# Where the passes over the output weights, some sums and the last two rows stand in a hybrid attention and RG-LRU block

## The chip, the cores and the metric

The kernel runs on one NeuronCore of a Trainium2 chip. The metric is the device time of one execution in microseconds; the kernel before takes 917.62 us (median of three runs, 917.18 to 918.01). The engines are called by short names: PE is TensorE, DVE VectorE, ACT ScalarE, POOL GpSimd and SP SyncE. Each engine works through its own instructions strictly in the order in which the program lists them, because the kernel switches the automatic ordering off (`manual_schedule`) and writes the order out by hand. Transfers are issued on SP's queue or on POOL's, a few on ACT's.

## The reference

The reference computes one layer of a hybrid block over 1024 positions and 1024 channels, all in float32. Cut to what matters here:

```
h      = rmsnorm(x, norm_g) * (1 + scale) + shift          # scale, shift, gate from c @ w_ada + b_ada
q, k, v, g_attn, xr, g_rnn, m_attn, m_rnn = split(h @ w_in)
y_attn = sliding_window_attention_with_sinks(rope(q), rope(k), v) * silu(g_attn)
y_rnn  = rg_lru(causal_depthwise_conv(xr)) * silu(g_rnn)
merged = sigmoid(m_attn) * (y_attn @ w_attn_proj) + sigmoid(m_rnn) * (y_rnn @ w_rnn_proj)
x      = x + gate * (merged @ w_out)
out    = rmsnorm(x, final_g)
```

The change touches the preparation of `w_out`, the product `merged @ w_out`, and the last normalisation.

## The kernel before, in words

**Products.** A float32 operand is split into a high part (rounded by ACT, a "cast") and a low part (the remainder, a subtraction on DVE, a "rest"); a product is three matmuls: high by high, low by high, high by low. The large products `h @ w_in` and `merged @ w_out` are made by a Strassen-Winograd scheme, seven block products in the place of eight, on operands that are sums of blocks.

**Stages.** After a start-up the projection runs as 22 `Pair`s of 128 output columns each, seven slots per pair, twelve matmuls per slot (line 694). A planner (`run`, `background`, `put`) walks through the slots; besides the fixed steps of a pair it takes steps from three waiting lists and puts each one where its own estimate of ACT's and DVE's load (`Load`) leaves room. A callable entry in a list holds the list back until it returns true. The last pair and the product with `w_rnn_proj` are woven into attention (a loop over `u` from 0 to 34). Then comes the product with `w_attn_proj` in eight chunks `c` of 48 matmuls (`ap_k`), with the merging of each chunk behind it: `merge1` and `merge2` on DVE, `naturals` (high and low part of a merged chunk), `sums` (Strassen sums of merged chunks `kc` and `kc + 4`). Beside it `prep_r` makes the cast and the rest of the next chunk's weights, which PE needs before it can start that chunk. The product with `w_out` follows, 24 groups `n` of 12 matmuls and then a row-wise end (`products`, line 1864).

**The weight passes.** `out_weights` prepares `w_out` in eight passes, four values of `kc` by two column halves. A pass has four steps: `load` (two 256 KB transfers from `w_out` into tiles `t1`, `t2`, issued on POOL), `gated` (two multiplications by the gate on DVE, line 1179, and two stores on POOL), `one` (two subtractions, lines 1184 and 1185, and a store) and `two` (an addition and a subtraction, lines 1189 and 1190, and a store). There is one set of tiles, so a pass's `load` stands behind the pass before. The stores go to `wq_d` in memory, and the product with `w_out` reads them back (`load_b11`, `load_wr`). The passes stand at the end of the third waiting list. In front of `gated`, `one` and `two` stands the function `idle`; in front of `load` it does not stand, only a delay in slots. What is left of the list when the pairs end goes, without the callables, into `rest_out`, and `outs(n)` issues the next `n` steps from it, at once and in order. Before, it is called at three places: after attention (as many steps as leave a whole number of passes, then one more), after `naturals(0)`, and after `naturals` of the chunks `c` = 2, 3, 4.

**The end.** The first four row blocks `x1` and the last four `x2` take the banks `b1` and `b2` of `merged @ w_out` by additions on DVE (`add_x`, line 1869), are squared on ACT (line 1883) and scaled (`row1`, `scale2`). `prep_sum` makes high and low parts of a Strassen sum for later groups; `prep_right(n + 4)` does the same for the weights four groups ahead. `scale2` scales one row block: its second half on ACT (line 1911), its first half on DVE (line 1912), then two stores.

Of the kernel before, what the change touches and what calls it, by code (L numbers as in the profile page):

```python
# [52 lines left out]
def tile_hybrid_block(ctx, tc, x, x_t, pk, rows, posr, posi, c_row, w_ss, w_gate, w_main, w_v,  # L53
# [525 lines left out]
    W = {}  # L579
# [104 lines left out]


    SLOT, GATE = 2.75, 5.5
    ROOMY = (52, 56), (111, 117)

    def product(ps, w, b, first=True):
        h, l = w  # L690
# [95 lines left out]
    def flush():  # L786
        while behind:
            behind.pop(0)()
# [126 lines left out]
                "C22": (half(1), lambda s: []),  # L915
                "C21": lambda s: other(s) + [("N", 0, 0, lambda: conv(1)(s))]}

    gq, asks = [], []

    def gate_weights(hb, oc):  # L920

# [16 lines left out]
    def ask(hb, oc):  # L938

        if ("g", (hb, oc)) not in W and (hb, oc) not in gq:  # L940
            gq.append((hb, oc))
        return ("g", (hb, oc)) in W
# [7 lines left out]
    def start_gates(hb):  # L950

        load1, split1 = gate_weights(hb, 1)
        c0, c1 = after_gates(hb, 0), after_gates(hb, 1)
        asks.extend([lambda: ask(hb, 0), lambda: ask(hb, 1)])
        waiting[0].extend([lambda: "gate" in W, asks[-2]])
        if hb < 3:
            one, two = [], [asks[-1]]
            for todo, steps_ in ((one, c0), (two, c1)):
                for i, step in enumerate(steps_):
                    todo.extend(step + [slots(1)])  # L960
                    if todo is one and i == 1:
                        todo.append(lambda: second(hb))
            waiting[0].extend(one + two)
        else:
            gap = [None]
            for item in ([[lambda: W.setdefault("rush", True)], c0[0], gap, c0[1],
                          [lambda: second(hb)], c0[2], c0[3], gap, c0[4], c0[5], gap, c0[6],
                          [lambda: ask(hb, 1)], c1[0], c0[7], gap, c0[8], c1[1], c0[9], c1[2],
                          c1[3], gap, c1[4], c1[5], gap, c1[6], c1[7], gap, c1[8], c1[9]]):
                waiting[0].extend([slots(1)] if item is gap else item)  # L970
        waiting[1].extend([load1, slots(2)] + split1)
        return True
# [186 lines left out]


    def idle():
        t = W["slot"]
        return t < 130 and (not waiting[0] or waiting[0][0] in asks or (
            any(a <= t < b for a, b in ROOMY) and Load.dve <= Load.pe + 2.8))

    def out_weights(kc, cols):
        t1, t2, t3, t4 = wq
# [97 lines left out]
    def sink(u):  # L1265
        px = at.tile([P, 4, P + 1], F32, tag="p", name="p", bufs=3)
        U["p", u] = px, at.tile([P, 2, 4], F32, tag="small", name="small", bufs=4)
        gs = slice(u // 8 * 4, u // 8 * 4 + 4)
        return lambda: G.tensor_copy(px[:, :, P:P + 1], W["sink"][:, gs].unsqueeze(2))
# [336 lines left out]
    def outs(n):  # L1606
        for _ in range(min(n, len(rest_out))):
            put(rest_out.pop(0)[0])
# [27 lines left out]
    for u in range(32 + 3):  # L1636
        todo = (left - KEEP + (35 - u) // 2) // (35 - u)
        if u < 32:
            scores(u)
            maxima_a(u)  # L1640
            maxima_d(u)
        if 1 <= u < 33:
            weights_a(u - 1)
        low = [steps_[2] for steps_ in high]
        while high:
            high.pop(0)[1]()
        for _ in range(todo):
            piece()
        flush()
        if 1 <= u < 33:  # L1650
            weights_d(u - 1)
        if u >= 3:
            values(u - 3)
            join_a(u - 3)
            join_d(u - 3)
        if 2 <= u < 34:
            transposed(u - 2)
            split_a(u - 2)
            split_d(u - 2)
        if u + 1 < 32:  # L1660
            sink(u + 1)()
        if 2 <= u < 34:
            masks(u - 2)
        if "hpool" in W:
            for f in low:
                f()
            if late and ("gq", late[0]) in U and u >= loaded[late[0]] + 2:
                high.append(a_prep(late.pop(0)))
                high[0][0]()
        do_later()  # L1670
        if u >= 3 and u % 2 == 0:
            late.append((u - 3) // 2)
        if u >= 2 and len(loaded) < 16 and len(loaded) <= (u - 2) // 2 and (
                len(loaded) - (late[0] if late else (u - 2) // 2) < 2):
            m = len(loaded)
            load_gq(m)
            loaded[m] = u
# [4 lines left out]
    for m in late:  # L1682
        for f in a_prep(m):
            f()
    flush()
    at_ctx.close()
    psx_ctx.close()
    outs((len(rest_out) - 1) % 4 + 1)
    for _ in more:
        pass  # L1690
    outs(1)
    flush()
    load_r(10)
    prep_r(9, 0)
# [82 lines left out]

    first_w = []

    def load_b11():  # L1780
        for kc in range(4):
            first_w.append(load_half(wq_d[kc][:, 0, :]))

    def load_wr(n):
# [13 lines left out]
    load_r(KC + 3)  # L1798
    ap_k(0, range(6))
    prep_r(KC + 1, 1)  # L1800
    merge1(0)
    merge_loads(1)
    merge_load2(1)
# [11 lines left out]
    for c in range(2, KC):  # L1815
        ps[c] = new_ps()
        ap_k(c, range(KC))
        if c + 2 < KC:
            load_r(KC + c + 2)
        if c + 1 < KC:  # L1820
            for i in range(2):
                prep_r(KC + c + 1, i)
        merge1(c)
        if c + 1 < KC:
            merge_loads(c + 1)
        merge2(c - 1)
        if c + 1 < KC:
            merge_load2(c + 1)
        naturals(c - 1)
        if c < 5:  # L1830
            outs(4)
        if c > 5:
            for n in ((0,), (1, 2, 3))[c - 6]:
                prep_right(n, first_w[n])
        if c in (5, 6):
            sums(c - 5)
        if c == 5:
            load_b11()
    load_wr("B21")
    load_wr("NT1")  # L1840
    load_wr("B22")
# [67 lines left out]
    def scale2(i, f, eng=nc.sync):  # L1909
        a, b = x2[i]  # L1910
        A.activation(b, b, AF.Copy, scale=f[:, 3:4])
        V.scalar_tensor_tensor(out=a, in0=a, scalar=f[:, 3:4], in1=fg_bc[:, SL[0]], op0=MUL,
                               op1=MUL)
        t = (4 + i) * P
        dma(out[t:t + P, SL[1]], b, eng)
        dma(out[t:t + P, SL[0]], a)

    for n in range(24):
        p, kc = n // 4, n % 4
        for i in range(4):  # L1920
            products(p, kc, i)
        if n == 0:
            naturals(7)
            for i in range(4):
                load_x1(i, "ss" if i > 1 else "xo", 2)
            fg_bc = W["tout"].tile([P, S], F32, tag="rp", name="fg_bc")
            dma(fg_bc[:], rows[0:1, D:2 * D].to_broadcast([P, D]))
        if n == 3:
            for i in range(4):
                A.copy(b1[i], b2[i])  # L1930
        if n + 4 < 28:
            prep_right(n + 4)
        if n in (2, 4):
            sums(2 if n == 2 else 3)
        if n == 4:
            for i in (2, 3, 0):
                load_x2(i)
        if n == 5:
            load_x2(1)
        at = {5: ("S1", 0), 7: ("S1", 1), 8: ("NS4", 0), 10: ("NS4", 1), 12: ("S2", 0),  # L1940
              14: ("S2", 1), 16: ("NS3", 0), 18: ("NS3", 1)}
        if n in at:
            prep_sum(*at[n])
        if n in (10, 12, 16):
            load_wr({10: "T2", 12: "NT3", 16: "NT4"}[n])
        if n == 7:
            for i in range(4):
                add_x(x1[i][:, SL[0]], b1[i], ADD)
            for i in range(4):
                square(x1[i][:, SL[0]], pcol(0, i))  # L1950
        if n == 11:
            for i in range(4):
                add_x(x2[i][1], b1[i], SUB)
        if n == 15:
            for i in range(4):
                add_x(x1[i][:, SL[1]], b1[i], SUB)
        if n == 19:
            for i in range(4):
                add_x(x1[i][:, SL[1]], b2[i], ADD)
            for i in range(4):  # L1960
                square(x1[i][:, SL[1]], pcol(4, i))
        if n in (9, 10):
            for i in (2 * n - 18, 2 * n - 17):
                TT(out=x1[i][:, SL[0]], in0=x1[i][:, SL[0]], in1=fg_bc[:, SL[0]], op=MUL)
        if n == 21:
            roots1()
        if n in (21, 22):
            for i in (2 * n - 42, 2 * n - 41):
                row1(i)
# [17 lines left out]
    for i in range(3):  # L1987
        f = fs[i]
        guard(f, pcol(8, i))
        for kc in range(4):  # L1990
            products(6, kc, i)
        add_x(x2[i][0], b2[i], ADD)
        square(x2[i][0], f[:, 1:2])
        if i < 2:
            root(f)
            scale2(i, f)
    f = small()
    last_cut(0, f)
    root(fs[2])
    TT(out=f[:, 5:6], in0=f[:, 4:5], in1=pcol(8, 3), op=ADD)  # L2000
    guard(f, f[:, 5:6])
    last_cut(1, f)
    scale2(2, fs[2])
    root(f)
    scale2(3, f, A)
    w_ctx.close()
    order.close()

# [78 lines left out]
```

## Time and profile before

| | us |
|---|---|
| median of three runs | 917.62 |
| the profiled execution, its own time | 915.79 |
| its span, first to last instruction | 914.1 |
| PE busy | 893.5 |
| DVE busy | 722.1 |
| ACT busy | 557.7 |
| POOL busy | 124.8 |

The granted clock of the profiled execution was 0.999. The span is 1.7 us shorter than that execution's own time, and the execution lies 1.8 us under the median. In the rows of the profile a line such as "742.41 0.42 DVE L1184" is start, duration, engine and source line; the bracket at its end gives how long the engine sat idle before it and what ended that. "x4" is a count. PE's matmuls are pipelined: their durations overlap, and what counts is from start to start.

### The profile page before, as it was taken

How to read it: one execution, taken by the hardware profiler on the slowest of the kernel's cores; microseconds unless marked ns; L12 is line 12 of the kernel's file. 1: busy time of each engine (PE TensorE's matmuls, PEld its weight loads, DVE VectorE, ACT ScalarE, POOL GpSimd, SP SyncE). 2: the span in 40 equal slices, each digit the busy share in tenths (PEclk: the TensorE clock that was granted, in tenths of full speed). 3: DMA queues.
4: the chain of work that ended last, by engine and by line, in shares of the span. 5: the costliest groups of instructions: out<-in, count | busy, mean ns of one | idle time of the engine just before them, and what ended most of it. 6: DMA issues, size and time to landing. Idle time of an engine off the chain costs nothing.

```text
span 914.1 us, 12609 instructions
## 1 busy us (share of the span) xinstructions
PE 893.5 (98%) x4187; PEld 740.2 (81%) x4187; DVE 722.1 (79%) x1143; ACT 557.7 (61%) x1088; POOL 124.8 (14%) x204
## 2 busy tenths in 40 slices
PE   5999999999999999999999999999999999999996
PEld 3779888887888788888887888888888888888785
DVE  7976889797679983988598476899999846779865
ACT  6753656454566755775678685888888631114555
POOL 0120000000010010000000001454453421310002
PEclk9999999999999999999999999999999999999999
DMA  9953458862344362346155257996666268878314
GB/s 354 414 191 112 174 164 308 280 235 84 116 141 152 116 235 83 115 157 218 47 185 174 83 196 255 334 355 221 215 207 205 73 205 324 306 259 333 110 46 184
DMA packets 88598, 182.05 MB, mean 199 GB/s; under 512 B 13891, under 2 KB 30275, under 8 KB 88534
## 3 DMA queue, kind: packets, MB, share of 16 engines
q1 hardware_dynamic: 81908, 161.57, 50.9%
q0 software_dynamic: 6336, 19.37, 6.0%
q8 instruction: 33, 0.54, 0.2%
q14 instruction: 31, 0.25, 0.1%
q10 hardware_dynamic: 290, 0.32, 0.1%
HBM read 124.49 MB, written 57.12 MB: 199 GB/s over the span
## 4 chain that ended last, share of the span: by engine, by line
PE 75%; DVE 9%; DMA 7%; issue 5%; ACT 3%; POOL 1%; SPq 0%; DVEq 0%; ACTq 0%; POOLq 0%
PE bk L694 42%; PE rp L174 7%; PE bo L1864 6%; PE pgate L989 5%; PE bk L174 3%; PE s_ps L1281 3%; PE pv L1353 2%; DMA wq_d<-wq 2%; DVE wl L110 2%; DMA wq<-w_out 2%; PE pt L1319 1%; PE pmain L174 1%; DMA wada<-w_ss 1%; DMA r<-w_main 1%; PE bk L1527 1%
## 5 line engine op out<-in xcount | busy, mean ns | idle before, releaser
L694 PE MATMUL bk<-nh,wl 128*128 128x512 f32 x352 | 137.4, 390 | 0.4 <-DVE wl L110 0.4
L694 PE MATMUL bk<-nh,wh 128*128 128x512 f32 x352 | 137.1, 389 | 0.0
L694 PE MATMUL bk<-nl,wh 128*128 128x512 f32 x352 | 137.0, 389 | 0.0
L110 DVE TENSOR_TENSOR wl<-r,wh 128x512 fp32r<-128x512 f32 x113 | 80.7, 728 | 9.0 <-ACT wh L104 9.0
L104 ACT CAST wh<-r 128x512 fp32r<-128x512 f32 x113 | 68.6, 619 | 22.5 <-PE bk L1527 12.2
L60 POOL DMA_DIRECT2D wq_d<-wq x32 | 21.9, 685 | 424.7 <-DVE wq L1179 379.5
L694 PEld LDWEIGHTS bk<-nh,wl 128*128 128x128 f32 x352 | 66.1, 188 | 15.2 <-DVE wl L110 1.5
L694 PEld LDWEIGHTS bk<-nh,wh 128*128 128x128 f32 x352 | 66.1, 188 | 13.8
L694 PEld LDWEIGHTS bk<-nl,wh 128*128 128x128 f32 x352 | 66.1, 188 | 13.5
L694 PE MATMUL bk<-hh,wl 128*128 128x512 f32 x176 | 68.6, 390 | 0.4 <-DVE wl L110 0.4
L694 PE MATMUL bk<-hh,wh 128*128 128x512 f32 x176 | 68.6, 390 | 0.0
L694 PE MATMUL bk<-hl,wh 128*128 128x512 f32 x176 | 68.5, 389 | 0.0
L110 DVE TENSOR_TENSOR wl<-ws,wh 128x512 fp32r<-128x512 f32 x76 | 51.9, 685 | 0.0
L1305 ACT ACTIVATE p<-p,small 128x129 f32<-128x129 f32 x128 | 50.1, 401 | 0.0
L104 ACT CAST wh<-ws 128x512 fp32r<-128x512 f32 x76 | 45.8, 614 | 0.1
L1864 PE MATMUL bo<-wh,sum 128*128 128x512 f32 x128 | 40.0, 391 | 0.9 <-DVE xo L1869 0.9
L694 PEld LDWEIGHTS bk<-hh,wh 128*128 128x128 f32 x176 | 33.0, 188 | 7.7 <-ACT wh L104 0.9
L694 PEld LDWEIGHTS bk<-hh,wl 128*128 128x128 f32 x176 | 33.0, 188 | 7.6 <-DVE wl L110 0.8
L694 PEld LDWEIGHTS bk<-hl,wh 128*128 128x128 f32 x176 | 33.0, 188 | 6.8
L1281 PE MATMUL s_ps<-ks,qs 128*128 128x256 f32 (+1 forms) x256 | 37.6, 289 | 0.2 <-DVE p L1295 0.2
L797 ACT ACTIVATE c<-bk 128x512 f32<-128x512 f32 x29 | 17.3, 596 | 29.7 <-PE bk L694 29.6
L694 PE MATMUL bk<-hha,wl 128*128 128x512 f32 x88 | 34.5, 392 | 0.6 <-DVE wl L110 0.5
(412 smaller groups left out, 2337.4 us busy)
## 6 DMA issues: line engine op xcount, KB each, us to landing
r<-w_main SPq DMA_DIRECT2D x100, 256.0 KB, 4.3
wada<-w_ss SPq DMA_DIRECT2D x16, 512.5 KB, 8.7
qs<-q_d SPq DMA_DIRECT2D x16, 512.0 KB, 6.4
wq_d<-wq POOLq DMA_DIRECT2D x24, 256.0 KB, 4.7
wr<-wq_d SPq DMA_DIRECT2D x24, 256.0 KB, 5.1
ks<-k_d SPq DMA_DIRECT2D x24, 192.0 KB, 5.3
wq<-w_out POOLq DMA_DIRECT2D x16, 256.0 KB, 5.5
q_d<-rhi SPq DMA_DIRECT2D x16, 256.0 KB, 4.0
```

The costliest lines, as they stand in the source:

```text
L60: return eng.dma_start(dst, src)
L104: A.copy(dst[0][:], src)
L110: V.tensor_tensor(out=dst[1][:], in0=src, in1=f32(dst[0][:]), op=ALU.subtract)
L174: mm = T.matmul(ps[hf], ww, xx[kc][hf], start=(kc == 0 and ww is w_h and xx is xh), stop=(kc == KC - 1 and xx is xl))
L694: W["pe"] = T.matmul(ps, ww[:, c], b[kc][xx_], start=(first and kc == 0 and i == 0), stop=(kc == 3 and i == 2), skip_group_check=not first)
L797: A.activation(t["t"], s(), AF.Tanh, scale=0.5)
L989: W["pe"] = T.matmul(ps[:, SL[hf]], ww[:, c0:c0 + P], xx_[:, SL[hf]], start=(ic == 0 and i == 0), stop=(ic == 1 and i == 2))
L1281: W["pe"] = T.matmul(o, qs[:, j, qc], ks[:, b, k0 + (0 if n else P):k0 + 256], start=(b == 0), stop=(b == 1))
L1305: A.activation(px[:, j, :], px[:, j, :], AF.Exp, bias=sm[:, 0, j:j + 1], accum_out=sm[:, 1, j:j + 1])
L1319: W["pe"] = T.transpose(pt[:, j, :], px[:, j, 0:P], ident[:])
L1353: W["pe"] = T.matmul(pv[:], b, m[:].rearrange("p j q -> p (j q)"), start=(i == 0), stop=(i == len(prods) - 1))
L1864: T.matmul(bank[p][i] if dst is None else dst, a[:, ts_], b[:][:, sl], start=(new and kc == 0 and j == 0), stop=(kc == 3 and j == 2), skip ...
```

## The change

1. `idle` no longer looks at the planner's load or at the waiting lists: it is true in the slots 52 to 55 and false otherwise. `ROOMY` and the list `asks` go.
2. `outs` is called at other places: one step in attention's loop at `u` = 32, ahead of `masks`; four after the loop; four ahead of `merge1(0)`; four after `naturals(0)` as before; four after `naturals` in the chunks `c` = 2, 3, 4, 5.
3. `sums(0)` and `sums(1)` move from the chunks 5 and 6 to the chunks 6 and 7; three of the four loads of `load_b11` stay in chunk 5, the fourth moves to chunk 6.
4. In the product with `w_out`, the second part of the sum S1 is made at group 8 in the place of 7, the first part of NS4 at 9 in the place of 8, and the multiplications of `x1`'s first half by `final_g` at the groups 13 and 14 in the place of 9 and 10.
5. `scale2` becomes a generator; the third row's scaling on ACT is issued ahead of the last row's second half, its part on DVE and its stores behind that.

```
-    ROOMY = (52, 56), (111, 117)
...
-    gq, asks = [], []
+    gq = []
...
-        asks.extend([lambda: ask(hb, 0), lambda: ask(hb, 1)])
-        waiting[0].extend([lambda: "gate" in W, asks[-2]])
+        waiting[0].extend([lambda: "gate" in W, lambda: ask(hb, 0)])
         if hb < 3:
-            one, two = [], [asks[-1]]
+            one, two = [], [lambda: ask(hb, 1)]
...
     def idle():
-        t = W["slot"]
-        return t < 130 and (not waiting[0] or waiting[0][0] in asks or (
-            any(a <= t < b for a, b in ROOMY) and Load.dve <= Load.pe + 2.8))
+        return 52 <= W["slot"] < 56
...
         if u + 1 < 32:
             sink(u + 1)()
+        else:
+            outs(u == 32)
         if 2 <= u < 34:
             masks(u - 2)
...
     flush()
+    outs(4)
     at_ctx.close()
     psx_ctx.close()
-    outs((len(rest_out) - 1) % 4 + 1)
     for _ in more:
         pass
-    outs(1)
     flush()
...
-    def load_b11():
-        for kc in range(4):
+    def load_b11(kcs):
+        for kc in kcs:
             first_w.append(load_half(wq_d[kc][:, 0, :]))
...
     prep_r(KC + 1, 1)
+    outs(4)
     merge1(0)
...
-        if c < 5:
+        if c < 6:
             outs(4)
         if c > 5:
             for n in ((0,), (1, 2, 3))[c - 6]:
                 prep_right(n, first_w[n])
+        if c > 5:
+            sums(c - 6)
         if c in (5, 6):
-            sums(c - 5)
-        if c == 5:
-            load_b11()
+            load_b11(range(3) if c == 5 else [3])
...
     def scale2(i, f, eng=nc.sync):
         a, b = x2[i]
         A.activation(b, b, AF.Copy, scale=f[:, 3:4])
+        yield
         V.scalar_tensor_tensor(out=a, in0=a, scalar=f[:, 3:4], in1=fg_bc[:, SL[0]], op0=MUL,
                                op1=MUL)
         t = (4 + i) * P
         dma(out[t:t + P, SL[1]], b, eng)
         dma(out[t:t + P, SL[0]], a)
+        yield
...
-        at = {5: ("S1", 0), 7: ("S1", 1), 8: ("NS4", 0), 10: ("NS4", 1), 12: ("S2", 0),
+        at = {5: ("S1", 0), 8: ("S1", 1), 9: ("NS4", 0), 10: ("NS4", 1), 12: ("S2", 0),
               14: ("S2", 1), 16: ("NS3", 0), 18: ("NS3", 1)}
...
-        if n in (9, 10):
-            for i in (2 * n - 18, 2 * n - 17):
+        if n in (13, 14):
+            for i in (2 * n - 26, 2 * n - 25):
                 TT(out=x1[i][:, SL[0]], in0=x1[i][:, SL[0]], in1=fg_bc[:, SL[0]], op=MUL)
...
             root(f)
-            scale2(i, f)
+            list(scale2(i, f))
...
     guard(f, f[:, 5:6])
+    third = scale2(2, fs[2])
+    next(third)
     last_cut(1, f)
-    scale2(2, fs[2])
+    next(third)
     root(f)
-    scale2(3, f, A)
+    list(scale2(3, f, A))
```

More of the change, by code (lines that the diff above doesn't have):

```diff
@@ L686, in tile_hybrid_block @@
     SLOT, GATE = 2.75, 5.5
-    ROOMY = (52, 56), (111, 117)
     def product(ps, w, b, first=True):
@@ L916, in xr_sinks @@
                 "C21": lambda s: other(s) + [("N", 0, 0, lambda: conv(1)(s))]}
-    gq, asks = [], []
+    gq = []
     def gate_weights(hb, oc):
@@ L953, in start_gates @@
         c0, c1 = after_gates(hb, 0), after_gates(hb, 1)
-        asks.extend([lambda: ask(hb, 0), lambda: ask(hb, 1)])
-        waiting[0].extend([lambda: "gate" in W, asks[-2]])
+        waiting[0].extend([lambda: "gate" in W, lambda: ask(hb, 0)])
         if hb < 3:
-            one, two = [], [asks[-1]]
+            one, two = [], [lambda: ask(hb, 1)]
             for todo, steps_ in ((one, c0), (two, c1)):
@@ L1161, in idle @@
     def idle():
-        t = W["slot"]
-        return t < 130 and (not waiting[0] or waiting[0][0] in asks or (
-            any(a <= t < b for a, b in ROOMY) and Load.dve <= Load.pe + 2.8))
+        return 52 <= W["slot"] < 56
     def out_weights(kc, cols):
@@ L1661, in tile_hybrid_block @@
             sink(u + 1)()
+        else:
+            outs(u == 32)
         if 2 <= u < 34:
@@ L1685, in tile_hybrid_block @@
     flush()
+    outs(4)
     at_ctx.close()
     psx_ctx.close()
-    outs((len(rest_out) - 1) % 4 + 1)
     for _ in more:
         pass
-    outs(1)
     flush()
@@ L1778, in tile_hybrid_block, with load_b11 @@
     first_w = []
-    def load_b11():
-        for kc in range(4):
+    def load_b11(kcs):
+        for kc in kcs:
             first_w.append(load_half(wq_d[kc][:, 0, :]))
@@ L1800, in tile_hybrid_block @@
     prep_r(KC + 1, 1)
+    outs(4)
     merge1(0)
@@ L1829, in tile_hybrid_block @@
         naturals(c - 1)
-        if c < 5:
+        if c < 6:
             outs(4)
@@ L1834, in tile_hybrid_block @@
                 prep_right(n, first_w[n])
+        if c > 5:
+            sums(c - 6)
         if c in (5, 6):
-            sums(c - 5)
-        if c == 5:
-            load_b11()
+            load_b11(range(3) if c == 5 else [3])
     load_wr("B21")
@@ L1911, in scale2 @@
         A.activation(b, b, AF.Copy, scale=f[:, 3:4])
+        yield
         V.scalar_tensor_tensor(out=a, in0=a, scalar=f[:, 3:4], in1=fg_bc[:, SL[0]], op0=MUL,
@@ L1916, in scale2 @@
         dma(out[t:t + P, SL[0]], a)
+        yield
     for n in range(24):
@@ L1939, in tile_hybrid_block @@
             load_x2(1)
-        at = {5: ("S1", 0), 7: ("S1", 1), 8: ("NS4", 0), 10: ("NS4", 1), 12: ("S2", 0),
+        at = {5: ("S1", 0), 8: ("S1", 1), 9: ("NS4", 0), 10: ("NS4", 1), 12: ("S2", 0),
               14: ("S2", 1), 16: ("NS3", 0), 18: ("NS3", 1)}
@@ L1961, in tile_hybrid_block @@
                 square(x1[i][:, SL[1]], pcol(4, i))
-        if n in (9, 10):
-            for i in (2 * n - 18, 2 * n - 17):
+        if n in (13, 14):
+            for i in (2 * n - 26, 2 * n - 25):
                 TT(out=x1[i][:, SL[0]], in0=x1[i][:, SL[0]], in1=fg_bc[:, SL[0]], op=MUL)
@@ L1995, in tile_hybrid_block @@
             root(f)
-            scale2(i, f)
+            list(scale2(i, f))
     f = small()
@@ L2001, in tile_hybrid_block @@
     guard(f, f[:, 5:6])
+    third = scale2(2, fs[2])
+    next(third)
     last_cut(1, f)
-    scale2(2, fs[2])
+    next(third)
     root(f)
-    scale2(3, f, A)
+    list(scale2(3, f, A))
     w_ctx.close()
```

## The prediction

> **What bounds the kernel now.** I read the page first, then PE's waits, then the stretch in which the change puts most of its work, chunk by chunk.
>
> ```profile
> span 914.1 us, 12609 instructions
> PE 893.5 (98%) x4187; PEld 740.2 (81%) x4187; DVE 722.1 (79%) x1143; ACT 557.7 (61%) x1088; POOL 124.8 (14%) x204
> ...
> PE bk L694 <- DVE wl L110: 1.3, 3, 0.5
> PE bo L1864 <- DVE xo L1869: 0.9, 2, 0.6
> PE bo L1864 <- DVE wl L110: 0.3, 1, 0.3
> ```
>
> PE is busy nearly throughout, and after the start its waits add up to little. The table by stretches (span, PE, PEld, DVE, ACT, POOL, each with a count) has the eight chunks of the product with `w_attn_proj`, cut where PE starts each; here chunk 6 and the sum:
>
> ```profile
> 806.69:817.57 10.88, 10.88 (x50) 9.01 (x48) 10.02 (x13) 2.19 (x4) 0.28 (x1) 1.00 0.78 268
> ...
> sum 87.05, PE 87.05 PEld 72.07 DVE 58.39 ACT 13.80 POOL 19.50; mean PE 10.88 PEld 9.01 DVE 7.30 ACT 1.72 POOL 2.44
> ```
>
> PE needs 10.88 us per chunk and never stands still from 741.40 to 828.45. But DVE carries 10.02 us in chunk 6, so PE's cover is thin, and the timeline of DVE shows how thin:
>
> ```profile
> 741.21 1.29 DVE L1179 TENSOR_TENSOR wq<-wq,gate_bc 128x512 f32<-128x512 f32 x2
> 742.41 0.42 DVE L1184 TENSOR_TENSOR wq<-wq 128x256 f32<-128x256 f32 x1
> ...
> 743.54 0.43 DVE L1190 TENSOR_TENSOR wq<-wq,wq 128x256 f32<-128x256 f32 x1
> 743.88 1.29 DVE L110 TENSOR_TENSOR wl<-r,wh 128x512 fp32r<-128x512 f32 x2
> 754.54 1.23 DVE L1731 SCALAR_TENSOR_TENSOR m<-smr,m 128x1024 f32<-128x1024 f32 x1 [9.38 <-DMA smr<-smr_d]
> ...
> 760.60 1.23 DVE L1731 SCALAR_TENSOR_TENSOR m<-smr,m 128x1024 f32<-128x1024 f32 x1 [3.62 <-DMA smr<-smr_d]
> ...
> 765.63 1.29 DVE L1179 TENSOR_TENSOR wq<-wq,gate_bc 128x512 f32<-128x512 f32 x2
> ...
> 768.30 1.28 DVE L110 TENSOR_TENSOR wl<-r,wh 128x512 fp32r<-128x512 f32 x2
> ...
> 773.80 0.69 DVE L1744 TENSOR_TENSOR hla<-m,hha 128x512 fp32r<-128x512 f32 x1 [0.69 <-ACT hha L1742]
> ...
> 801.83 0.69 DVE L1179 TENSOR_TENSOR wq<-wq,gate_bc 128x512 f32<-128x512 f32 x1 [4.34 <-DMA wq<-w_out]
> 803.78 0.69 DVE L1179 TENSOR_TENSOR wq<-wq,gate_bc 128x512 f32<-128x512 f32 x1 [1.26 <-DMA wq<-w_out]
> ...
> 805.86 1.29 DVE L110 TENSOR_TENSOR wl<-r,wh 128x512 fp32r<-128x512 f32 x2
> ```
>
> ```profile
> 796.67 1.14 ACT L104 CAST wh<-r 128x512 fp32r<-128x512 f32 x2
> ...
> 750.02 0.39 PE L174 MATMUL pmain<-ah,wl 128*128 128x512 f32 x1
> ...
> 807.14 0.39 PE L174 MATMUL rp<-ah,wl 128*128 128x512 f32 x1
> ```
>
> The last lines of each are the heart of the case. ACT had cast chunk 6's weights by 797.8; their rests could have followed. They stood on DVE behind `gated`, which waited for its load from `w_out`, until 805.86. The first was ready at about 806.5, and PE used it at 807.14. So a wait of `gated` holds DVE's whole queue, and behind it stand the rests that PE needs.
>
> **Which steps are left.** The first edit decides that. Multiplications of `gated` by stretch, and POOL after the first pass:
>
> ```profile
> 255.00:280.00 25.00, 1.29 (x2) 1.00 0.55 184
> 280.00:460.00 180.00, 2.58 (x4) 1.00 0.40 138
> ...
> 740.00:812.00 72.00, 6.64 (x10) 1.00 0.85 299
> ```
>
> ```profile
> 274.06 1.45 POOL L60 DMA_DIRECT2D wq<-w_out  x2
> ```
>
> Each pass has two. So before, one pass ran between 255 and 280, two more up to 460, five at the end. The first falls into the slots 52 to 55 and stays; the two after it move to the end, with eight stores and four loads of 0.73 us on POOL, which is idle enough there (19.50 of 87.05). But `load` has no `idle` in front of it: the second pass's load follows the first pass by a slot (274.06), and still will. So 27 steps are left (three of the second pass, four each of six), and the list begins with `gated`, not with `load`. The new calls take 1, 4, 4, 4, 4, 4, 4 and 2 of them. The single step at `u` = 32 is `gated`; each of the next six calls is therefore `one`, `two`, `load`, `gated`, the load directly ahead of the `gated` that needs it. Before, every call of four was `gated`, `one`, `two`, `load`, with a chunk's DVE work between load and use.
>
> **What one such call costs DVE.** From the start s of `one`: `two` ends at s + 1.56 (742.41 to 743.97). How fast POOL follows, and how long loads take:
>
> ```profile
> 742.79 2.74 POOL L60 DMA_DIRECT2D wq_d<-wq  x4 [7.24 <-DVE wq L1179]
> ...
> 783.62 1.45 POOL L60 DMA_DIRECT2D wq<-w_out  x2
> ```
>
> ```profile
> wq<-w_out POOLq DMA_DIRECT2D x8, 256.0 KB, 6.3
> ```
>
> ```profile
> DMA to landing us min/median/max: 3.8/4.2/4.7
> ```
>
> ```profile
> DMA to landing us min/median/max: 7.6/7.6/7.6
> ```
>
> POOL starts 0.3 after DVE's result (742.50 to 742.79) and needs 0.73 per issue, so `two`'s store goes at s + 1.86, the loads at s + 2.6 and s + 3.3. Landing is 6.3 in the median of this stretch; the last two rows are the extremes, the two loads issued at 783.62 behind stores while SP was quiet (3.8 and 4.7), and the one at 749.37 among SP's loads (7.6). The second multiplication starts when the second load is in and holds DVE 0.6. A call lasts L = 4.0 + landing, between 7.8 and 11.6, where the old six instructions took 2.67 (741.21 to 743.88). I take a landing of 6.7 for the first call, amid the loads after attention; 4.7 for the second, when SP waits for `merge1`; 5.3 for the four others, between the pair most like them and the median. That is 10.7, 8.7 and four times 9.3.
>
> **DVE's new schedule.** The first call starts at 741.2, plus 0.7 for the step at `u` = 32, priced below: 741.9 to 752.6. Two rests (0.6 each): 753.8; PE wanted the first at 750.0 and stands some 3 us. Second call to 762.5. `merge1(0)` (1.2), then the next `smr`, which cannot be loaded sooner and took 4.8 (755.77 to 760.60): 768.5. From there 5.0 to the next call (760.60 to 765.63): 773.5 to 782.8. Each further chunk has 6.1 of rests, merges and naturals (768.30 to 774.41) and a call, 15.4 against PE's 10.88: the calls end at 798.2, 813.6 and 829.0. The last is followed by chunk 6's first rest, ready at 829.7. Before, PE used it at 807.14 (chunk start plus two matmuls). So PE reaches chunk 6 **22.5 us late**, having stood about 3, 6, 4.5, 4.5 and 4.5 us. Chunk 5 has only `one` and `two`; chunk 7's rest is ready by 838, before chunk 6 ends at 840, and PE runs on. In general the delay is the sum of the six L less 34.1; the bounds 7.8 and 11.6 give 13 and 36.
>
> **The small terms.** At `u` = 32, `gated`'s stores stand on POOL ahead of `masks`:
>
> ```profile
> 727.05 0.63 POOL L1339 TENSOR_SCALAR_AFFINE_SELECT phm<-phc 128x512 fp32r<-128x512 f32 x1 [2.41 <-ACT phc L1324]
> 728.05 0.76 POOL L1339 TENSOR_SCALAR_AFFINE_SELECT plm<-plc 128x512 fp32r<-128x512 f32 x1 [0.37 <-DVE plc L1330]
> ...
> 731.62 0.40 PE L1353 MATMUL pv<-plm,dv 128*128 128x512 f32 x1
> ```
>
> `gated` takes DVE from 727.9 to 729.1, the stores POOL to 730.8, the masks 1.4: `plm` at 732.3 against 731.6, **+0.7**, in the 22.5 already.
>
> Additions ahead of rests, and the sum of S1 behind them:
>
> ```profile
> 849.51 1.29 DVE L1764 TENSOR_TENSOR sum<-m,sum 128x512 fp32r<-128x512 f32 x2
> 850.71 2.47 DVE L1869 TENSOR_TENSOR xo<-xo,bo 128x512 f32<-128x512 f32 x4
> ...
> 860.38 1.29 DVE L1964 TENSOR_TENSOR xo<-xo,fg_bc 128x512 f32<-128x512 f32 x2
> ```
>
> The first additions lose the 1.2 of the sum ahead of them, the second the 1.2 of multiplications. Both waits of PE on them go: 0.9 shown, and 0.16 each that a matmul's shown 0.39 hides over the 0.227 between starts (10.88 / 48): **-1.2** (bounds 0 and -1.2). The 0.3 that PE waited for a rest behind them, 0.5 with the hidden part, goes too, as chunk 5 has no `sums` any more: **-0.5**. But `sums(1)`, four instructions of 0.7, now stands ahead of `merge2(7)`, and so ahead of the rests for group 4: +2.9 if nothing covers it, 0 if PE's four groups of 2.7 us do; I take **+0.5**. The multiplications at the groups 13 and 14 lie beside PE's groups, and so does the fourth load of `load_b11`, a chunk later and still a chunk early: 0, at worst the 1.2 of a pair of multiplications.
>
> The end:
>
> ```profile
> 908.06 0.70 ACT L1911 ACTIVATE r<-r,fst 128x512 f32<-128x512 f32 x1
> 908.67 0.28 ACT L1892 ACTIVATE fst<-fst 128x1 f32<-128x1 f32 x1
> ```
>
> The third row's scaling leaves the place between the last square and the last root, 0.6, and delays the square by 0.1: **-0.4** (bounds 0 and -0.6).
>
> PE after a standstill has a lower pace, seen only at the start, in the chain: four matmuls in 1.92 where four of 0.227 take 0.91.
>
> ```profile
> 16.25 1.92 PE pmain L439 x4
> ```
>
> Only in chunk 6, behind the last standstill, does that reach the end; earlier it is hidden in PE's next wait. **+1.0** (0 to 2). The Trainium skill (TensorE: Matmul & The Clock Gate, HAM oscillation) says that a PE gap longer than about 3.4 us halves its clock until it has been busy about as long again; by that the term would be 1.7, an estimate, and the sum 0.7 higher. The chain's row agrees in kind.
>
> The two passes that leave the pairs take 2.67 us of DVE each from beside PE's matmuls; at most the 1.3 us of PE's waits for rests there (three, first block) could go with them; one such wait more would cost 0.5, the longest of the three. I take 0.
>
> Sum: 22.5 - 1.2 - 0.5 + 0.5 - 0.4 + 1.0 = 21.9. The profiled execution's own 915.79 (span 914.1 and 1.7 around it) becomes 937.7; it lies 1.8 under the median, so 917.62 becomes **939.5**.
>
> **Rivals.**
>
> *The loads stay a call ahead.* If 28 steps are left, the list begins with `load`, that goes out at `u` = 32, and each call is again `gated`, `one`, `two`, `load`. Then DVE keeps its pace, and only -1.2 - 0.5 - 0.4 remain, and +0.7 for two issues on POOL ahead of the masks: 916.2, not slower. For it: eight calls have room for 28. Against: the load at 274.06, which nothing in the new `idle` holds back. It decides from one step more or less. 0.07.
>
> *Loads land fast.* A cycle of 15 us moves the bytes of 11, so the queues are emptier: landing 3.8 everywhere, each L 7.8, delay 12.7, the other terms -0.6, time 929.7. For it the row 3.8/4.2/4.7; against it the median of 6.3. 0.2.
>
> *Loads land slowly*, sharing the engines with SP's burst at each chunk (`smr`, `sma`, weights, `m`): 7.6, L 11.6, delay 35.5, time 952.5. For it the row 7.6; against it that PE's standstill thins the burst. 0.13.
>
> **How the numbers follow.** The forecast has 0.6, around it 934 to 945. The range reaches to both DMA cases and leaves out the first rival and the edges: 927 to 951. This measurement tells 0.2% (1.8 us) from no change. Slower holds 0.6 + 0.2 + 0.13 = 0.93; the first rival's 916.2 lies near the border, so 0.04 same and 0.03 faster.
>
> **What would show it.** In the changed profile: two multiplications of `gated` in the pairs, two near 728, twelve in the end; in each of six calls POOL's loads directly ahead of them, and DVE idle 5 to 8 us before them, released by the load, some 40 us in all (six times L less 2.7) against the 4.34, 1.26 and their like of before; PE's idle time by DVE's `wl` near 20 us at chunks 1, 3, 4, 5 and 6; PE's waits on line 1869 gone. I am wrong if POOL issues a load at `u` = 32, if DVE's idle time ahead of `gated` is short, or if PE's chunks start without gaps.

## The result, and the profile after

The changed kernel takes **940.66 us** (median; 939.27 to 941.95), the kernel before 917.56 beside it: ratio 1.0252, 95% interval 1.0239 to 1.0265, or 23.1 us more. The profiled execution took 940.59, with a span of 938.9: 24.8 over the 914.1 of before. The forecast was 939.5.

PE's waits after the change (us in total, times, longest) have two new lines at their head:

```profile
PE pmain L174 <- DVE wl L110: 11.9, 3, 4.3
PE rp L174 <- DVE wl L110: 8.3, 2, 4.6
PE bk L387 <- DVE xt L381: 6.7, 1, 6.7
...
PE bk L693 <- DVE wl L110: 1.3, 3, 0.5
```

Five waits, 20.2 us, all for rests of weights in the product with `w_attn_proj`. The three waits of the first block (1.3) are unchanged, and no line names the additions to x (now line 1867) any more. The multiplications of `gated` (now line 1175), by stretch as before, show where the passes went:

```profile
225.00:280.00 55.00, 1.30 (x2) 1.00 0.39 132
280.00:460.00 180.00, 0.00 (x0) 1.00 0.38 127
...
700.00:735.00 35.00, 1.28 (x2) 1.00 0.38 126
735.00:812.00 77.00, 5.48 (x8) 0.93 0.70 239
812.00:940.00 128.00, 2.72 (x4) 0.97 0.54 191
```

Two in the pairs, two near 728, twelve at the end. The page's group of them (busy, mean ns | idle time of DVE ahead of them and what ended it) and DVE's timeline, cut to three of the six calls:

```profile
L1175 DVE TENSOR_TENSOR wq<-wq,gate_bc 128x512 f32<-128x512 f32 x16 | 10.8, 691 | 44.5 <-DMA wq<-w_out 44.4
```

```profile
751.80 0.69 DVE L1175 TENSOR_TENSOR wq<-wq,gate_bc 128x512 f32<-128x512 f32 x1 [9.44 <-DMA wq<-w_out]
...
799.20 1.32 DVE L1175 TENSOR_TENSOR wq<-wq,gate_bc 128x512 f32<-128x512 f32 x2 [7.62 <-DMA wq<-w_out]
800.44 1.29 DVE L110 TENSOR_TENSOR wl<-r,wh 128x512 fp32r<-128x512 f32 x2
...
831.09 1.40 DVE L1175 TENSOR_TENSOR wq<-wq,gate_bc 128x512 f32<-128x512 f32 x2 [6.76 <-DMA wq<-w_out]
832.41 1.29 DVE L110 TENSOR_TENSOR wl<-r,wh 128x512 fp32r<-128x512 f32 x2
```

DVE stands idle 44.4 us for the loads. In five of the six calls the rests of line 110 follow directly behind; in the second, `merge1(0)` stands between. POOL's timeline shows the first loads leaving beside the call that needs them:

```profile
728.46 1.32 POOL L60 DMA_DIRECT2D wq_d<-wq  x2 [4.24 <-DVE wq L1175]
729.80 0.66 POOL L1335 TENSOR_SCALAR_AFFINE_SELECT phm<-phc 128x512 fp32r<-128x512 f32 x1
730.39 0.64 POOL L1335 TENSOR_SCALAR_AFFINE_SELECT plm<-plc 128x512 fp32r<-128x512 f32 x1
...
743.38 1.58 POOL L60 DMA_DIRECT2D wq<-w_out  x2
...
758.61 0.73 POOL L60 DMA_DIRECT2D wq<-w_out  x1 [1.49 <-DMA wq_d<-wq]
```

At 728.46 POOL issues stores, not a load; the loads go out at 743.38, behind the stores of `two`, and DVE waits for them until 751.80. The transfers issued between 741 and 746 (count, size, median us from issue to landing):

```profile
wq<-w_out POOLq DMA_DIRECT2D x2, 256.0 KB, 8.4
m<-tr_d SPq DMA_DIRECT2D x1, 512.0 KB, 9.6
...
sma<-sma_d SPq DMA_DIRECT2D x1, 512.0 KB, 10.8
```

The pair lands 8.4 us after its issue, amid SP's loads of 512 KB. PE's timeline at the third standstill and the last:

```profile
796.87 0.61 PE L174 MATMUL rp<-ah,wh 128*128 128x512 f32 x2
801.18 0.74 PE L174 MATMUL rp<-ah,wl 128*128 128x512 f32 x2 [3.70 <-DVE wl L110]
...
813.37 0.61 PE L174 MATMUL pmain<-ah,wh 128*128 128x512 f32 x2
817.41 0.73 PE L174 MATMUL pmain<-ah,wl 128*128 128x512 f32 x2 [3.43 <-DVE wl L110]
...
833.15 1.22 PE L174 MATMUL rp<-ah,wl 128*128 128x512 f32 x2 [4.57 <-DVE wl L110]
834.17 1.05 PE L174 MATMUL rp<-al,wh 128*128 128x512 f32 x2
...
856.01 0.39 PE L1862 MATMUL bo<-wh,hha 128*128 128x512 f32 x1
...
932.20 0.28 PE L1862 MATMUL bo<-wh,hl 128*128 128x256 f32 x1
```

And the same two points, the first and the last matmul of the product with `w_out`, before:

```profile
828.45 0.39 PE L1864 MATMUL bo<-wh,hha 128*128 128x512 f32 x1
...
906.69 0.28 PE L1864 MATMUL bo<-wh,hl 128*128 128x256 f32 x1
```

So the 24.8 us add up. Chunk 6's first rest is used at 833.15 instead of 807.14: +26.0. From there to the product with `w_out` take 22.86 (to 856.01) instead of 21.31 (to 828.45): +1.55, PE's lower pace. That product takes 76.19 from its first matmul to its last instead of 78.24: -2.05. From the last matmul to the end of the span are 6.7 us (938.9 - 932.2) instead of 7.4 (914.1 - 906.7): -0.7. The sum is 24.8.

### The profile page after: what moved, and what is told of

Its sections match the earlier page's. It is cut to its first block, busy times and chain, and to the rows that moved or that the text cites. A ratio compares the mean times of both kernels' runs of the same rounds, so it can differ in the third digit from the quotient of the medians.

```text
span 938.9 us, 12615 instructions
## 1 busy us (share of the span) xinstructions
PE 900.1 (96%) x4187; PEld 744.4 (79%) x4187; DVE 722.3 (77%) x1143; ACT 557.8 (59%) x1088; POOL 125.2 (13%) x204
## 4 chain that ended last, share of the span: by engine, by line
PE 76%; DVE 8%; DMA 7%; issue 4%; ACT 3%; POOL 1%; SPq 0%; DVEq 0%; POOLq 0%; ACTq 0%
PE bk L693 41%; PE rp L174 8%; PE bo L1862 7%; PE pgate L987 5%; PE bk L174 3%; DMA wq<-w_out 3%; PE s_ps L1277 3%; PE pv L1349 2%; PE pmain L174 2%; DMA r<-w_main 2%; DVE wl L110 1%; PE pt L1315 1%; DMA wada<-w_ss 1%; PE bk L1523 1%; PE bk L1522 1%
## 5 line engine op out<-in xcount | busy, mean ns | idle before, releaser
L1175 DVE TENSOR_TENSOR wq<-wq,gate_bc 128x512 f32<-128x512 f32 x16 | 10.8, 691 | 44.5 <-DMA wq<-w_out 44.4
L1739 ACT CAST hha<-m 128x512 fp32r<-128x512 f32 x4 | 2.5, 620 | 63.8 <-DVE m L1734 63.8
```

The source lines that it names most:

```text
L1175: TT(out=t[:], in0=t[:], in1=gate_bc[:, :, cols], op=ALU.mult)
```

## The experiments

The first four kernels below were timed on one chip, beside a kernel before of 916.86; the other four together as well, beside one of 917.07.

**The order in the calls.** One step less in the call after attention; from then on each call is `gated`, `one`, `two`, `load`, as it was before.

```diff
     flush()
-    outs(4)
+    outs(3)
     at_ctx.close()
```

> The changed kernel with one number altered: the call of outs after attention issues three steps in the place of four, so that every later call is gated, one, two, load, and each load again stands a call ahead of its use. The passes stay where the change put them (one among the pairs, seven at the end). Theory (the whole loss is DVE's queue held by gated, which waits for the load directly ahead of it): no PE wait for rests at the chunks 1, 3, 4, 5, 6, and only the gains of the small edits stay: 914.5 to 916 us. Rival (the two passes moved to the end cost by their DVE and POOL work itself, or by the traffic they add there): at least 5 us over the kernel before, 922 us or more.

Measured: 919.48, ratio 1.0037 (1.0024 to 1.0049). No step and no byte is gone, only the order is another, and by the ratios 20 of the 23 us go with it. So the order causes most of the loss; but 919.5 is between the two expectations, 3.5 above the theory's. What is left is in PE's waits, three at the product with `w_out` (line 1862) and one for a rest at chunk 6, where the theory had none:

```profile
PE bo L1862 <- ACT bo L1930: 1.4, 1, 1.4
...
PE bo L1862 <- ACT wh L104: 1.2, 1, 1.2
...
PE rp L174 <- DVE wl L110: 0.7, 1, 0.7
PE bo L1862 <- DVE wl L110: 0.4, 1, 0.4
```

and, ahead of it, in DVE's timeline and POOL's:

```profile
751.38 0.69 DVE L1175 TENSOR_TENSOR wq<-wq,gate_bc 128x512 f32<-128x512 f32 x1 [7.08 <-DMA wq<-w_out]
...
781.22 0.69 DVE L1175 TENSOR_TENSOR wq<-wq,gate_bc 128x512 f32<-128x512 f32 x1 [5.64 <-DMA wq<-w_out]
...
803.80 0.69 DVE L1175 TENSOR_TENSOR wq<-wq,gate_bc 128x512 f32<-128x512 f32 x1 [3.85 <-DMA wq<-w_out]
```

```profile
774.34 1.45 POOL L60 DMA_DIRECT2D wq<-w_out  x2 [3.50 <-DMA wq_d<-wq]
```

The load comes a chunk ahead in the program, but it fills the tiles from which the stores of the pass before still read. POOL holds it until these have landed (3.50), and DVE then waits 5.64 for what left at 774.34. A load "a call ahead" is not a whole call ahead. DVE is idle 20.2 us ahead of `gated` here, against 44.4 after the change and 10.9 in the same stretch before. Of PE's two waits for ACT the longer shows how this lateness is passed on. DVE ends the last merge 11.3 us into the product with `w_out` (840.97 against 829.65), where it was 6.9 before; ACT's cast of that chunk waits for it, and the copies of line 1930 stand behind the cast (ACT's timeline):

```profile
841.01 1.14 ACT L1739 CAST hh<-m 128x512 fp32r<-128x512 f32 x2 [6.26 <-DVE m L1734]
```

**No loads.** The six loads at the end are left out, with all else in place; the six passes work on what the tiles happen to hold.

```diff
+    rest_out = [[("S", 0, 0, lambda: None)] if g[0][0] == "S" else g for g in rest_out]
```

> The changed kernel without the six loads from w_out at the end: gated, one, two and all stores stay, in the changed order, on what the tiles happen to hold, so six of eight passes prepare wrong weights. Theory (what costs is the wait for the load, not the order of the steps): each call falls from about 10 us of DVE to 2.7, PE's waits for rests at the end go, 914.5 to 916.5 us. Rival (one and two ahead of gated, or POOL's stores between, hold DVE by themselves): more than 925 us.

Measured: 913.33, ratio 0.9967 (0.9956 to 0.9978), and no wait of PE at the end. The work of two passes more at the end costs nothing; all that the change loses goes with the loads. This run takes away their bytes as well as the wait for them; the last run below keeps the bytes.

**Without the move of the passes.** The kernel before, with all other edits of the change (sums, additions, last rows); a part of them here, the lines on the sums stand further below.

```diff
-        at = {5: ("S1", 0), 7: ("S1", 1), 8: ("NS4", 0), 10: ("NS4", 1), 12: ("S2", 0),
+        at = {5: ("S1", 0), 8: ("S1", 1), 9: ("NS4", 0), 10: ("NS4", 1), 12: ("S2", 0),
...
-        if n in (9, 10):
+        if n in (13, 14):
...
-    scale2(2, fs[2])
+    next(third)
```

> The kernel before with only the small edits: sums one chunk on and load_b11 split, additions ahead of rests with S1, NS4 and the multiplications of x1 moved, and the end of the last two rows. The weight passes stay as before. Theory: PE's waits of 0.5 at group 1, 0.85 at group 8 and 0.55 at group 12 go, and the end is 0.4 to 0.7 shorter: 2.3 to 2.6 us less than before, about 915.1. Rival (these waits only pass to the next late thing, as sums(1) stands ahead of merge2(7)): within 0.5 us of before.

Measured: 914.13, ratio 0.9976 (0.9967 to 0.9985): 2.2 us faster by the ratio (1.4 to 3.0). The other edits are a gain, as the sum had them; the move of the passes alone costs the rest, 2.8% (1.0252 / 0.9976) or some 25 us.

**The parts of that gain.** The order of the last two rows alone:

```diff
         A.activation(b, b, AF.Copy, scale=f[:, 3:4])
+        yield
...
+    third = scale2(2, fs[2])
+    next(third)
     last_cut(1, f)
-    scale2(2, fs[2])
+    next(third)
```

> The kernel before with only the new order of the last two rows. Theory: the last root follows the last square directly; 0.4 to 0.7 us less than before, 917.0. Rival (the end is set by the last stores' landing, not by ACT): no difference.

Measured: 916.48, ratio 1.000 (0.999 to 1.001). The total decides nothing: 0.4 is less than it tells. The profiles do show the edit: from the start of the last matmul to the end of the span are 6.8 us here, and 6.7 or 6.8 in every kernel with this edit, against 7.4 in the three without it (the kernel before and the next two).

The additions ahead of the rests alone, the lines of `at` and `(13, 14)` above:

```diff
-        at = {5: ("S1", 0), 7: ("S1", 1), 8: ("NS4", 0), 10: ("NS4", 1), 12: ("S2", 0),
+        at = {5: ("S1", 0), 8: ("S1", 1), 9: ("NS4", 0), 10: ("NS4", 1), 12: ("S2", 0),
...
-        if n in (9, 10):
+        if n in (13, 14):
```

> The kernel before with the additions to x ahead of the rests alone (the sum of S1 behind them at groups 8 and 9, the multiplications at groups 13 and 14). Theory: the two waits of PE on the additions, 0.9 shown and 1.2 with the part that a matmul's length hides, go: -1.2 to -1.6, 915.3 to 916 where the kernel before has 916.9 to 917.6. Rival (the waits only move to the next rest): within 0.4 of before.

Measured: 915.57, ratio 0.9985 (0.9976 to 0.9993): -1.4 us by the ratio. The time is as the theory had it. PE's waits from 735 us on:

```profile
PE rp L174 <- DVE wl L110: 1.5, 1, 1.5
PE bo L1864 <- DVE wl L110: 0.4, 1, 0.4
```

The waits on the additions are gone. The 1.5, at chunk 6, stands where the edit doesn't reach. There the second multiplication of `gated`, held by its load, starts at 806.03 (803.78 before), and the rests follow at 808.11: it is the wait behind `gated` that these kernels share. Its length differs between profiles: 1.5 as well in the run of the last two rows, whose program is that of before up to there, 0.6 in the kernel without the move of the passes, and no line at all before.

The sums a chunk on alone:

```diff
...
+        if c > 5:
+            sums(c - 6)
         if c in (5, 6):
-            sums(c - 5)
-        if c == 5:
-            load_b11()
+            load_b11(range(3) if c == 5 else [3])
```

> The kernel before with the sums one chunk on and the fourth load of B11 with them, alone. Theory: PE's wait for a rest at group 1, 0.3 shown and 0.5 hidden part included, goes, and the second sums ahead of the last merge cost up to 0.5 at group 4: -0.5 to 0. Rival (the second sums hold up the rests of group 4 in the open): +0.5 to +2.9.

Measured: 916.21, ratio 0.9995 (0.9986 to 1.0003). It cannot be told from no change; the 0.5 to 2.9 of the rival doesn't show, and PE's waits have no line for a rest at the product with `w_out`.

**A dose.** The aligned order from the third call on; two calls stay `one`, `two`, `load`, `gated`.

```diff
     naturals(0)
-    outs(4)
+    outs(3)
```

> The changed kernel with three steps instead of four in the call behind the first naturals: only the first two calls are still one, two, load, gated; from then on each call is gated, one, two, load, a chunk between load and use. A dose of the cause. Theory (DVE's queue held by a load that was just issued, once per call): the standstill of PE at chunk 1 stays at about 4 to 5 us, the one at chunk 3 at 0 to 4.5, those at chunks 4, 5 and 6 go but for what the loads behind stores still cost there: 922 to 927. Rival (the cost comes from the bytes and issues that the end has more of, not from the order): no lower than 935. Rival (only the later calls cost, since DVE catches up after the first two): 919 to 920, as with all calls in the other order.

Measured: 921.13, ratio 1.0044 (1.0031 to 1.0058). That is 0.9 under the theory's range and 1.1 over the third expectation; the second (no lower than 935) falls. PE's timeline shows one standstill and what it drags behind it:

```profile
749.50 0.61 PE L174 MATMUL pmain<-ah,wh 128*128 128x512 f32 x2
754.13 1.22 PE L174 MATMUL pmain<-ah,wl 128*128 128x512 f32 x2 [4.02 <-DVE wl L110]
755.15 1.05 PE L174 MATMUL pmain<-al,wh 128*128 128x512 f32 x2
...
757.71 0.63 PE L174 MATMUL pmain<-al,wh 128*128 128x512 f32 x1
```

The standstill at chunk 1 stays, the one at chunk 3 is gone altogether: once PE is late, the second call's wait is covered. So the cost isn't so much per call; it is what DVE needs in total beyond what PE does meanwhile. The span is 4.9 longer (919.0 against 914.1), and this adds up: the product with `w_out` begins 6.7 later (835.16 against 828.45), by the 4.0 of the standstill and 2.6 of lower pace behind it; it takes 1.1 less, with a wait of 0.5 for ACT left in it; and the end is 0.7 shorter. The theory's place was right; its range was a little too high.

**The bytes without the wait.** The changed kernel with a second pair of tiles for every other pass, in room that is free until the product with `w_out`, and each load one pass earlier in the list.

```diff
-        t1, t2, t3, t4 = wq
...
+        t3, t4 = wq[2:]
...
+        def tiles():
+            t = W["wq2"] if kc and not cols.start else wq[:2]
+            return t, [t_[:, i, :] for t_ in t for i in range(2)]
...
+    for i in [3] + list(range(7, len(rest_out), 4)):
+        rest_out.insert(max(3, i - 3), rest_out.pop(i))
...
-    outs(4)
+    outs(2)
     at_ctx.close()
...
     tpool = pool(ctx, "tpool", bufs=2)
+    wq2 = tpool.tile([P, D], F32, tag="gate", name="wq2", bufs=1)
+    W["wq2"] = [wq2[:, SL[i]].rearrange("p (a t) -> p a t", a=2) for i in range(2)]
+    outs(2)
```

> The changed kernel, all its passes at the end as they are, with the loads of every other pass put into a second pair of tiles (the room of the second x2 row, free until the product with w_out), and each load one pass earlier in the list: gated, one, two, load of the pass after the next. Traffic and DVE's work are those of the changed kernel; no load waits for the stores of the pass before it, and none is used in the call that issues it. Theory (only the wait of gated for its load costs, and the same wait, shortened, is what the order gated, one, two, load with one pair of tiles still pays): no standstill of PE in the product with w_attn_proj, no wait of gated over 3 us, 913 to 915, as without the loads. Rival (the traffic of the loads, or two passes more at the end, cost by themselves): 917 to 920, as with one pair of tiles.

Measured: **913.01** (912.94 to 913.48), ratio 0.9960 (0.9947 to 0.9974), 3.7 us faster than before by the ratio. All six loads (twelve transfers) and all stores are there. PE's waits in the whole span:

```profile
PE bk L387 <- DVE xt L381: 7.6, 2, 7.2
PE bk L246 <- DMA r_bc<-c_row: 2.3, 1, 2.3
PE bk L693 <- DVE wl L110: 1.3, 3, 0.5
PE pmain L174 <- ACT hh L513: 0.9, 2, 0.7
```

None of them lies in the product with `w_attn_proj` or behind it. DVE's timeline still has one long wait, ahead of the first pass of the new order:

```profile
743.13 1.29 DVE L110 TENSOR_TENSOR wl<-r,wh 128x512 fp32r<-128x512 f32 x2 [0.47 <-ACT wh L104]
750.95 0.69 DVE L1180 TENSOR_TENSOR wq<-wq,gate_bc 128x512 f32<-128x512 f32 x1 [6.52 <-DMA wq<-w_out]
...
769.72 1.29 DVE L1180 TENSOR_TENSOR wq<-wq,gate_bc 128x512 f32<-128x512 f32 x2
```

That refutes "no wait over 3 us", but not the theory: at 743.13 chunk 1's rests are already done, and nothing that PE needs soon stands behind the 6.52. POOL, too, still holds loads for stores, by up to 5.02:

```profile
787.30 0.73 POOL L60 DMA_DIRECT2D wq<-w_out  x1 [5.02 <-DMA wq_d<-wq]
```

These are the stores from the load's own tiles, just issued; but the load's use lies a whole pass further on, and so the wait is covered: ahead of `gated` DVE is idle 10.2 us in all, where it was 20.2 with one set of tiles. Traffic costs nothing that shows here; the wait, with rests behind it, does.

This version has the lowest time of all. It and the kernel without the move of the passes (914.13) were timed beside different runs of before, and the intervals of their ratios touch, so that it beats that one too is likely and not shown.

## Why the prediction was right, step by step

- **27 steps, the load directly ahead of its `gated`: right.** POOL stores at 728.46 and loads at 743.38; 2, 2 and 12 multiplications. The rival of 28 steps didn't occur. Its price was also too low: the first experiment has that order in all but the first steps and is by its ratio 3.4 slower than the kernel before, where the rival had 1.4 faster, since loads a call ahead can still come late.
- **DVE's queue is what costs: right.** Five standstills of PE at the chunks named, 20.2 us in place of "near 20"; idle time ahead of `gated` 44.4 instead of some 40. The single standstills are 4.29, 4.20, 3.70, 3.43 and 4.57, where it had 3, 6, 4.5, 4.5 and 4.5. PE reaches chunk 6 later than the 20.2 alone would make it, because it also lost some 5 us to the lower pace behind the first three. Another order, no loads, or other tiles each remove the standstills.
- **What one call costs: right in kind, 0.8 us too small per call.** From `one` to the end of `gated` the six calls take 12.5, 9.4, 9.4, 10.4, 10.1 and 9.6: 61.4 in place of 56.6. The largest miss is the first (10.7): its loads needed 8.4 to land in the median, more than the slowest of before in that row (7.6). In the second, POOL held the loads 1.49 for stores, a wait that the working left out. By the prediction's own formula 61.4 - 34.1 gives 27.3; measured are 26.0. The formula has the first call begin at 741.9, and it began at 740.81: that 1.1 is most of the difference, and by luck it offset a part of the miss per call.
- **+0.7 at `u` = 32: absent.** The masks stand right behind the stores, as said, but the stores were through at 729.8, not 730.8 (the first left after the first multiplication), and the masks at 731.0, not 732.3.
- **The lower pace after a standstill, +1.0: 1.55.** Behind 833.15 two matmuls take 0.85 (834.17 to 835.02) where they take 0.45 at the full pace. The granted clock was 0.50 from 832.84 to 836.26; PE worked in 3.11 us of that, and half of it is the 1.55. The 1.7 by the rule of the Trainium skill (TensorE: Matmul & The Clock Gate, HAM oscillation) was nearer than the value taken from the start-up's row. In the dose run it cost more, 2.6 (13 matmuls at wider intervals from 754.13 to 759.67, less 0.227 each), because the clock stayed low twice as long (last section).
- **Additions, sums, group 4: -1.2 in sum, -2.05 measured.** The three waits are gone as said; the +0.5 for the sums ahead of `merge2(7)` isn't there, and in the run of the sums alone it doesn't show either. The waits were also larger than priced: from start to start the matmuls at these three places came 0.53, 0.85 and 0.55 late before, 1.9 in all where the sum had 1.7, since the next matmul also starts some 0.1 late. After the change no interval in this product is over 0.3. Some 0.1 stays unexplained.
- **The end, -0.4: -0.7** in the profile after, -0.55 in that of the edit alone, and by itself below what the timing tells.
- **The pairs, 0: right.** PE's waits there are the same 1.3.

The sum was 21.9. With its own terms as measured it is 26.0 + 1.55 - 2.05 - 0.7 = 24.8. The forecast in medians came nearer (939.5 to 940.66) because the profiled execution of before was 1.8 under its median and that of after was not under its own: part of the agreement is luck. The profile of before lacks the wait of 1.5 at chunk 6 that the same stretch of program shows in the run of the last two rows; that this made it 1.8 short is possible and not shown.

## What to carry to other kernels

Cutting a list of steps into calls of n is a schedule: one step more or less ahead of it decides whether a load and its first use fall into one call or a call apart, and so look at which pair of steps meets, not at how many there are. On an engine that runs in order, price a wait by what is queued behind it, not by its length: 6.52 us cost nothing with the rests done, while with the rests behind waits of 5.7 to 9.4 us made PE stand still for 3.4 to 4.6 us each. A prefetch into tiles that stores still read is only as early as those stores land; with a second set of tiles, in room that is free at that time, the load may wait for its stores and still be early, because its use lies a pass further on.

## What the runs showed of the hardware

- After a standstill of PE of 3.70, 4.02, 4.20, 4.29 and 4.57 us its matmuls of 512 columns came every 0.427 us instead of 0.227, for 3.1 to 5.5 us, which cost 1.55 to 2.6 us each; after one of 3.43 (817.41) they soon came every 0.227 again. The profile shows the granted clock at one half in these stretches; the last one of the changed kernel, then the one of the dose run (stretch, its length, PE, PEld, DVE, ACT and POOL, clock, DMA share, GB/s):

```profile
832.84:836.26 3.42, 3.11 (x7) 2.48 (x8) 3.38 (x5) 0.00 (x0) 0.66 (x1) 0.50 0.41 137
```

```profile
752.63:759.45 6.82, 5.32 (x13) 4.15 (x14) 3.33 (x7) 0.00 (x0) 3.49 (x6) 0.50 0.94 375
```

The four low stretches of the changed kernel begin at 754.34, 785.06, 802.12 and 832.84 and last 3.41 us each; the one of the dose run begins within its standstill and lasts twice that. The four starts lie 9, 5 and 9 times 3.41 us apart, so the clock seems to be set on a fixed grid, and where a standstill lies on the grid may count as much as its length. The Trainium skill's rule (the section named above) puts the limit at about 3.4 us. The five longer standstills agree with it, and the one of 3.43 is too near it to tell; that the limit lies between 3.43 and 3.70, or that length alone decides, isn't shown.

- A kernel with two passes' work more at the end is not slower (913.0 and 913.3), though DVE was at 10.02 of 10.88 us in chunk 6: over the eight chunks it was busy 58.39 of 87.05, and the 5.3 us of two passes (2.67 each) fit into the rest.
